# Row operations of two inverses on GpSimd, modulation's rows among the projections, and a written order for the recurrence's links

## The chip, the core and the metric

The kernel runs on one core of a Trainium2 chip. A core has four engines that compute: TensorE (PE, matrix products into PSUM), VectorE (DVE), ScalarE (ACT) and GpSimd (POOL); SyncE (SP) issues most of the loads. Each engine works through its own queue in order, and a semaphore holds an instruction until what it needs is there. The metric is the time of one execution on the device, in microseconds. Of the kernel before, three runs took 1595.9, 1590.84 and 1588.16 us; the median is 1590.84.

## The reference, cut to what matters

Two transformer blocks work one after the other on 512 tokens of width 1024, in float32. The change touches the first block alone, and in it the modulation, the projections and a recurrence over 256 context tokens and then 512 tokens:

```python
mod = silu(c) @ ada_w + ada_b                       # 6 x 1024 numbers: shifts, scales, gates
sh1, sc1, g1, sh2, sc2, g2 = split(mod, 6)
hx = rms_norm(x) * (1 + sc1) + sh1                  # the same for ctx
cb, cc, cx, r, k, v, w_lo, a_lo, g_lo = split(hx @ w_in)
for d in range(2):                                  # forward and backward in time
    decay = exp(-exp(-0.5) * sigmoid(w0[d] + tanh(w_lo) @ w_up[d]))
    a = sigmoid(a0[d] + a_lo @ a_up[d])
    k_d = k * (1 + (a - 1) * k_a)
    for t in time:                                  # S: 64 x 64, for each of 8 heads
        S = S * decay_t - (S @ kk_t) (kk_t * a_t)^T + v_t k_d_t^T
        y_t += S @ r_t
out = concat(cb * conv3(cc * cx), (groupnorm(y) + bonus) * gate) @ w_out
x = x + g1 * out
# then a gated convolutional FFN, the second block, a final norm
```

## The kernel before

Channels lie on the 128 partitions and tokens run along the free axis. A product with full float32 accuracy is made of three products of split operands (`mm3`, lines 169 to 171). A weight piece is loaded on SP's queue, copied by ScalarE to its high part `whi` and subtracted by VectorE to its low part `wlo` (`wsplit`, `split`, lines 181 and 182).

The work around the change has three stretches.

*Projections* (`proj`, about 45 to 260 us). `tile_of(u)` multiplies one block of 128 output columns of `w_in`, in two weight pieces of 512 rows each. The order is block 24, then 16 to 19 (`k`), 12 to 15 (`r`), then `v`, 25, and for each j of four the blocks 4+j, 8+j and j for the convolution. In between, the generator `prep` makes what the recurrence needs for head pair 0 and most of it for pair 1.

*Preparation and inverse* (`prep`, `inverse`). There are four head pairs j; 128 partitions hold the two heads of one. `prep(j)` computes decays and keys for direction 0 and then 1: products `pl` (lines 576, 577) through one PSUM buffer of tag `mm`, element operations on VectorE and ScalarE, and last the products `pa`, copied into the tile `AK` (line 636). `inverse(j)` then inverts 24 unit triangular matrices of 64 x 64, in blocks of 32: VectorE transposes `AK` to `U`; a loop over k of 31 rows makes one multiplication (line 671) and one subtraction (line 672) each on (31-k) x (k+1) elements of a partition; VectorE transposes the result `X` twice; products `pt` read `AK` again, products `po` follow (lines 691, 698 and 699), through one PSUM buffer of tag `inv`, and ScalarE copies `po` to `XT`. `AK` exists once, so the copies of the next pair into it wait until `pt` has read it.

*Recurrence* (`rwkv`, `stage`, about 260 to 520 us). A stage is one head pair. It goes through 12 chunks of 64 tokens in each of two directions d, each a chain of links: `pr` (product), `R` (ScalarE's copy, line 757), `pu` with `XT`, `U` (line 759), `p3`, and `S0` (line 769), the state which the next chunk's `pr` reads. From the fifth chunk on (the 512 tokens of the block itself) there is also `py`, the output, copied to `Y`. All four products of a direction go to parts of one PSUM bank, `C1[d]`. A helper `pair` makes, for two chunks at a time, the masked matrices (`psc`, to `AS` by VectorE, line 731) and transposed keys (`pkt`, to `kbt` by ScalarE). The group norm of a finished stage (`gn`) runs beside the next one; it starts with GpSimd's product `vt` x `bo` (line 789). Preparation's steps are put between the links by priorities; a planner orders each engine's queue by these and by what is ready. Where a tile's buffer is used again, the new tile waits for the old one's readers.

After stage 1 the preparation's memory is freed. Stages 2 and 3 then have `ada12` beside them (lines 528 to 542): the 4096 modulation numbers that the later parts need, as 32 products of a row of the transposed `ada_w` with `silu(c)`, each summed over 1024 elements by one VectorE operation (line 539), each row a load of 512 KB. Last, two groups of output products (`first`, `px`, 7 of 8 input blocks each) are issued beside the group norm of stage 3.

PSUM has eight banks. In the recurrence four are `sc` (`psc`, `pkt` and the group norm's products), two `C1`, one `mm` and one `inv`.

Of the kernel before, what the change touches and what calls it, by code (L numbers as in the profile page):

```python
# [122 lines left out]
class K:  # L123
# [10 lines left out]
    psa = None  # L134
# [38 lines left out]
    def psax(self, n=512, name="px"):  # L173
        return (self.psa or self.ps).tile([P, n], F32, tag="ax", name=name, bufs=self.axbufs)
# [124 lines left out]
    def proj(self):  # L299
# [45 lines left out]
        piece = lambda u, k0: self.wsplit(A["win"][u][:, k0:k0 + 4], 4, P)  # L345
# [108 lines left out]
        for j in range(4):  # L454
# [13 lines left out]
            for _ in range(self.RC):  # L468
                next(self.todo, None)

# [7 lines left out]
    def rwkv(self, es, ep):  # L478
# [4 lines left out]
        self.S0 = [st(f"S0{d}", [64]) for d in range(2)]  # L483
        self.C1 = [self.ps2.tile([P, 512], F32, name=f"c1{d}") for d in range(2)]
        for t in (*self.AS[0], *self.AS[1]):
            nc.vector.memset(t, 0.0)
        todo, gn = self.todo, iter(())
        for j in range(4):
            if j < 2:
                todo = chain(todo, self.prep(j + 2))  # L490
            gn = self.stage(j, self.S[j], todo, self.RB[j], gn)
            if j == 1:
# [26 lines left out]
    def first(self):  # L519
        self.ahead = []  # L520
        for n in range(2):
# [3 lines left out]
    def ada12(self):  # L525

        nc, wp = self.nc, self.wp
        tags = [("w", self.wbufs), ("whi", self.wsbufs), ("wlo", self.wsbufs)]
        cb, sb = (wp.tile([P, 1024], F32, tag=tags[i][0], name="cb", bufs=tags[i][1]) for i in (1, 2))
# [5 lines left out]
        for n in range(32):  # L535
            yield
            w, t = (wp.tile([P, 1024], F32, tag=tags[i][0], name="adaw", bufs=tags[i][1]) for i in (0, 2))
            nc.sync.dma_start(out=w, in_=self.A["adat"][n])
            nc.vector.scalar_tensor_tensor(out=t, in0=w, scalar=1.0, in1=cb, op0=ALU.mult, op1=ALU.mult, accum_out=acc[:, n:n + 1])
# [110 lines left out]
    def inverse(self, j):  # L650
# [14 lines left out]
        nc.gpsimd.memset(X.rearrange("p a b -> p (a b)")[:, ::33], 1.0)  # L665
        for k in range(31):
# [4 lines left out]
            nc.vector.tensor_tensor(out=tv, in0=U[:, k + 1:32, k:k + 1].to_broadcast([P, n, w]), in1=X[:, k:k + 1, 0:w].to_broadcast([P, n, w]), op=ALU.mult)  # L671
            nc.vector.tensor_tensor(out=X[:, k + 1:32, 0:w], in0=X[:, k + 1:32, 0:w], in1=tv, op=ALU.subtract)
# [12 lines left out]
        ps = lambda name: self.psp.tile([P, 12, 32], F32, tag="inv", name=name, bufs=1)  # L685
# [18 lines left out]
    def stage(self, j, S, todo, rb, gn):  # L704
# [5 lines left out]
        chunk = lambda d, g: g if d == 0 else (3 - g if g < 4 else 15 - g)  # L710
        cells = {}
        base = self.tc.cur_priority
        id2 = self.c("id2")

        def pair(i, d):

            c0 = min(chunk(d, 2 * i), chunk(d, 2 * i + 1))
            x = c0 >= 4
            W, N = (P, 192) if x else (64, 64)
            kr, kb = S["KR"][d], S["KB"][d]  # L720
            A = self.AS[d][i % 3]
            o = 256 + (c0 - 4) * P if x else c0 * 64
            ps = self.ps2.tile([P, 2, N], F32, tag="sc", name="psc", bufs=4)
            pt = self.ps2.tile([P, 2, 2, 64], F32, tag="sc", name="pkt", bufs=4)
            krs = [kr[:, o + c * W:o + c * W + W] for c in range(2)]
            for c in range(2):
                self.mmh(ps[:, c, 0:W], kb[:, c0 + c, d], krs[c])
                if x:
                    self.mmh(ps[:, c, W:N], kb[:, c0 + c, 1 - d], krs[c][:, 64:P])
            m = self.c(f"m{d}").bitcast(I32)[:, 0:N]  # L730
            nc.vector.copy_predicated(A[:, :, 0:N], m.unsqueeze(1).to_broadcast([P, 2, N]), ps)
            for c in range(2):
                for i in range(2):
                    self.mmh(pt[:, c, i], kb[:, c0 + c, i ^ d], id2)
            kt = r2.tile([P, 2, 2, 64], F32, tag="kbt", name="kbt", bufs=6)
            self.copy(nc.scalar, kt, pt)
            for c in range(2):
                cells[d, c0 + c] = (A[:, c], kt[:, c], krs[c], x)

        for g in range(12):  # L740
            at = base + self.PK * g
            with self.prio(at):
                if g % 2 == 0:
                    for d in range(2):
                        pair(g // 2, d)
                for d in range(2):
                    c = chunk(d, g)
                    A, kt, KR, x = cells.pop((d, c))
                    V, S0 = vt[:, c, :], self.S0[d]
                    R, U = (self.RU[d][g % 2][:, i, :] for i in range(2))  # L750
# [646 lines left out]
```

## Time and profile before

| | |
|---|---|
| three runs, median | 1590.84 us |
| the profiled execution | 1591.34 us, span 1589.5 us |
| busy in the span: PE, DVE, ACT, POOL | 94%, 63%, 40%, 8% |
| projections, 45 to 260 us: PE busy | 208.0 of 215 us |
| recurrence, 260 to 520 us: PE busy | 230.2 of 260 us |
| granted clock of TensorE over the span | 0.972 |

The span is the time from the first to the last instruction of the profiled execution; the execution itself takes 1.8 us more. Idle time of an engine counts only where another waits for it. Matrix products overlap in the engine, so a PE that is shown busy may still issue products more slowly than it could. In the rows below "waited for" is the event that came last; a wait for several events is put down to that one.

### The profile page before, as it was taken

The page shows a single profiled execution, that of the slowest core. Times are in us where ns is not written, and L with a number is a line of the kernel's source. Part 1 is how long each engine was busy: PE and PEld are TensorE (multiplying, and loading weights), DVE is VectorE, ACT ScalarE, POOL GpSimd, SP SyncE. Part 2 cuts the span into 40 slices and gives each one's busy share as a digit, 9 for nine tenths or more (in the row PEclk, how much of TensorE's full clock was granted, in tenths as well). Part 3 has the DMA queues.
Part 4 walks back from the last instruction along what each step waited for, and adds up shares of the span by engine and source line. Part 5 has one row for each costly group of instructions (what it writes and reads, how often), then busy time and mean ns, then how long its engine had stood idle before and what let it go on. Part 6 is the DMA issues. An engine that isn't in the chain of part 4 may idle for free. (4 is left out here: it accounts for less than half of the span.)

```text
span 1589.5 us, 28932 instructions
## 1 busy us (share of the span) xinstructions
PE 1498.6 (94%) x12062; PEld 1228.9 (77%) x12062; DVE 999.9 (63%) x1691; ACT 632.7 (40%) x1258; POOL 121.7 (8%) x141
## 2 busy tenths in 40 slices
PE   4899999989888999999999997999999999999998
PEld 2777787877777898888888875887677888888886
DVE  3436765777867669888863448588965555554221
ACT  3524343555453334333332325335554333333122
POOL 1111001020110000000000004121200000000000
PEclk9999898989999999999999998999999999999999
DMA  9243321010057613223323322211112222233221
GB/s 339 87 156 104 100 89 60 4 45 5 15 197 258 214 40 119 94 93 101 98 83 100 96 93 70 80 54 54 36 59 93 93 93 93 93 94 106 93 92 54
DMA packets 62179, 152.83 MB, mean 96 GB/s; under 512 B 12640, under 2 KB 14432, under 8 KB 62048
## 3 DMA queue, kind: packets, MB, share of 16 engines
q1 hardware_dynamic: 58016, 143.95, 27.9%
q10 hardware_dynamic: 4032, 7.04, 1.3%
q8 instruction: 94, 1.54, 0.4%
q14 instruction: 37, 0.30, 0.1%
HBM read 143.10 MB, written 7.86 MB: 95 GB/s over the span
## 5 line engine op out<-in xcount | busy, mean ns | idle before, releaser
L181 ACT ACTIVATE whi<-w 128x1024 fp32r<-128x1024 f32 (+2 forms) x220 | 208.7, 950 | 448.2 <-PE pm L170 333.3
L182 DVE TENSOR_TENSOR wlo<-w,whi 128x1024 fp32r<-128x1024 f32 (+2 forms) x212 | 229.9, 1086 | 201.3 <-ACT whi L181 195.3
L169 PE MATMUL pm<-ahi,whi 128*128 128x512 f32 (+1 forms) x624 | 236.4, 379 | 3.0 <-DVE sh L1080 2.6
L170 PE MATMUL pm<-alo,whi 128*128 128x512 f32 (+1 forms) x624 | 234.8, 376 | 0.0
L171 PE MATMUL pm<-ahi,wlo 128*128 128x512 f32 (+1 forms) x624 | 234.0, 375 | 0.0
L170 PE MATMUL pm<-al,whi 128*128 128x512 f32 x352 | 139.7, 397 | 0.0
L169 PE MATMUL pm<-ah,whi 128*128 128x512 f32 x352 | 139.2, 395 | 0.0
L171 PE MATMUL pm<-ah,wlo 128*128 128x512 f32 x352 | 139.2, 395 | 0.0
L169 PEld LDWEIGHTS pm<-ahi,whi 128*128 128x128 f32 x624 | 117.6, 189 | 24.2 <-ACT sh L1095 3.0
L171 PEld LDWEIGHTS pm<-ahi,wlo 128*128 128x128 f32 x624 | 117.6, 188 | 20.6 <-issue 0.7
L170 PEld LDWEIGHTS pm<-alo,whi 128*128 128x128 f32 x624 | 117.7, 189 | 20.3 <-issue 0.7
L953 DVE SCALAR_TENSOR_TENSOR cv<-pm,vec,cv 128x441 f32<-128x441 f32 (+2 forms) x176 | 121.1, 693 | 4.1
L170 PEld LDWEIGHTS pm<-al,whi 128*128 128x128 f32 x352 | 66.2, 188 | 16.1 <-issue 0.2
L171 PEld LDWEIGHTS pm<-ah,wlo 128*128 128x128 f32 x352 | 66.2, 188 | 16.1 <-issue 0.2
L169 PEld LDWEIGHTS pm<-ah,whi 128*128 128x128 f32 x352 | 66.2, 188 | 16.0
L171 PE MATMUL pm<-hhi,wlo 128*128 128x512 f32 x176 | 70.8, 402 | 2.7 <-DVE wlo L182 2.7
L169 PE MATMUL pm<-hhi,whi 128*128 128x512 f32 x176 | 71.4, 406 | 0.2 <-ACT whi L181 0.2
L170 PE MATMUL pm<-hlo,whi 128*128 128x512 f32 x176 | 70.6, 401 | 0.0
L169 PE MATMUL pd<-whi,gh 128*128 128x512 f32 x176 | 69.5, 395 | 0.0
L169 PE MATMUL pm<-hh,whi 128*128 128x512 f32 x176 | 69.3, 394 | 0.0
L170 PE MATMUL pm<-hl,whi 128*128 128x512 f32 x176 | 69.3, 394 | 0.0
L171 PE MATMUL pm<-hh,wlo 128*128 128x512 f32 x176 | 69.3, 394 | 0.0
(397 smaller groups left out, 3073.6 us busy)
## 6 DMA issues: line engine op xcount, KB each, us to landing
w<-in_fup SPq DMA_DIRECT2D x44, 512.0 KB, 3.7
adaw<-in_adat SPq DMA_DIRECT2D x32, 512.0 KB, 4.6
w<-in_win SPq DMA_DIRECT2D x44, 256.0 KB, 2.9
w<-in_wg SPq DMA_DIRECT2D x22, 512.0 KB, 3.6
w<-in_wu SPq DMA_DIRECT2D x22, 512.0 KB, 3.6
w<-in_wd SPq DMA_DIRECT2D x22, 512.0 KB, 3.7
w<-in_win SPq DMA_DIRECT2D x18, 512.0 KB, 3.5
w<-in_wout SPq DMA_DIRECT2D x16, 512.0 KB, 3.8
```

The costliest lines, as they stand in the source:

```text
L169: nc.tensor.matmul(out, lh, rh, start=(first and i == 0), stop=False)
L170: nc.tensor.matmul(out, lh, rl, start=False, stop=False)
L171: nc.tensor.matmul(out, ll, rh, start=False, stop=(last and i == n - 1))
L181: self.nc.scalar.activation(out=hi, in_=src, func=AF.Copy)
L182: (eng or self.nc.vector).tensor_tensor(out=lo, in0=src, in1=hi.bitcast(F32), op=ALU.subtract)
L953: nc.vector.scalar_tensor_tensor(out=o, in0=p[:, ro[0] + dr:ro[1] + dr, co[0] + dc:co[1] + dc], scalar=w(i), in1=o, op0=ALU.mult, op1=ALU.add)
```

## The change

It has six parts. They keep every product of the recurrence and every row operation.

- The loop of `inverse` runs on GpSimd for head pairs 2 and 3, and on VectorE for 0 and 1 as before.
- `ada12` moves into the projections: its first step and its 32 rows are drawn by `tile_of`, one for each of the blocks 12 to 24 and two for each of 25 and 0 to 11. Its tiles are a `cb` and two buffers `row` of its own. The second weight piece of blocks 0 to 11 and 25 gets its low part from GpSimd.
- `pair` becomes a generator `look` over all four stages. It is drawn by the links, eight steps ahead at the start and four for each chunk, so it also works on the next stage's chunks.
- All products of links and `look` carry one order token on PE, so they are issued in program order. In a chunk: `pr` of both directions, `R` of both, three steps of `look`, `pu` of both, `U` of both, the two parts of `p3` without `U`, one step of `look`, `p3` with `U`, the states, then `py`, whose copies to `Y` wait for the next chunk. The state gets two buffers a direction.
- `pr` and `p3` use the bank `C1[d]`, `pu` and `py` a second bank `C2[d]`. For the two banks, `sc` has three buffers instead of four, and the inverse's products share the one buffer of tag `mm` with preparation (the tag `inv` goes).
- Of the two early groups of output products, the second is issued at the start of the tail, in a bank of the next pool; tiles of tag `ax` alternate between the two pools.

```diff
-        return (self.psa or self.ps).tile([P, n], F32, tag="ax", name=name, bufs=self.axbufs)
+        pools = self.psa or [self.ps]
+        self.axn += 1
+        return pools[self.axn % len(pools)].tile([P, n], F32, tag="ax", name=name, bufs=self.axbufs // len(pools))
...
-        piece = lambda u, k0: self.wsplit(A["win"][u][:, k0:k0 + 4], 4, P)
+        piece = lambda u, k0: self.wsplit(A["win"][u][:, k0:k0 + 4], 4, P, eng=nc.gpsimd if k0 and not 12 <= u < 25 else None)
...
+        ada = self.ada12()
+
+        def rows(n):
+            for _ in range(n):
+                next(ada, None)
+
         def tile_of(u, x=True, c=True):
+            rows(1 if 12 <= u < 25 else 2)
...
+        for _ in ada:
+            pass
...
-        self.S0 = [st(f"S0{d}", [64]) for d in range(2)]
-        self.C1 = [self.ps2.tile([P, 512], F32, name=f"c1{d}") for d in range(2)]
+        self.S0 = [[st(f"S0{d}{i}", [64]) for i in range(2)] for d in range(2)]
+        self.C1, self.C2 = [[self.ps2.tile([P, 512], F32, name=f"c{i}{d}") for d in range(2)] for i in (1, 2)]
...
+        self.cells, self.vt, self.ahd = {}, {}, self.look()
+        self.load_v(0)
+        for _ in range(8):
+            next(self.ahd)
+        self.outs = []
...
-                todo = chain(self.splits(), self.ada12(), self.first())
+                todo = chain(self.splits(), self.first())
                 self.e3 = es.enter_context(ExitStack())
-                self.psa = self.psum(self.e3, "psa", side="right")
+                self.psa, self.axbufs = [self.psum(self.e3, "psa", side="right")], 1
...
-        for n in range(2):
+        for n in range(1):
...
-        tags = [("w", self.wbufs), ("whi", self.wsbufs), ("wlo", self.wsbufs)]
-        cb, sb = (wp.tile([P, 1024], F32, tag=tags[i][0], name="cb", bufs=tags[i][1]) for i in (1, 2))
+        row = lambda name: wp.tile([P, 1024], F32, tag="row", name=name, bufs=2)
+        cb, sb = wp.tile([P, 1024], F32, name="cb"), row("sb")
...
-            w, t = (wp.tile([P, 1024], F32, tag=tags[i][0], name="adaw", bufs=tags[i][1]) for i in (0, 2))
+            w = row("adaw")
...
+        e = nc.vector if j < 2 else nc.gpsimd
...
+            e.tensor_tensor(out=tv, in0=U[:, k + 1:32, k:k + 1].to_broadcast([P, n, w]), in1=X[:, k:k + 1, 0:w].to_broadcast([P, n, w]), op=ALU.mult)
+            e.tensor_tensor(out=X[:, k + 1:32, 0:w], in0=X[:, k + 1:32, 0:w], in1=tv, op=ALU.subtract)
...
-        ps = lambda name: self.psp.tile([P, 12, 32], F32, tag="inv", name=name, bufs=1)
+        ps = lambda name: self.psp.tile([P, 12, 32], F32, tag="mm", name=name, bufs=1)
...
+    def look(self):
+
         nc, r2 = self.nc, self.r2
-        XT = S["XT"]
-        vt = r2.tile([P, 12, 64], F32, tag="vt", name="vt", bufs=2)
-        nc.sync.dma_start(out=vt, in_=self.vD[:, j])
+        id2 = self.c("id2")
+        for j in range(4):
+            for i in range(6):
+                S = self.S[j]
+                x = i >= 2
+                W, N = (P, 192) if x else (64, 64)
+                part = []
+                for d in range(2):
+                    c0 = min(self.CH(d, 2 * i), self.CH(d, 2 * i + 1))
+                    kr, kb = S["KR"][d], S["KB"][d]
+                    o = 256 + (c0 - 4) * P if x else c0 * 64
+                    part.append((c0, kb, [kr[:, o + c * W:o + c * W + W] for c in range(2)], self.AS[d][i % 3]))
+                for d, (c0, kb, krs, A) in enumerate(part):
+                    ps = self.ps2.tile([P, 2, N], F32, tag="sc", name="psc", bufs=3)
+                    for c in range(2):
+                        if c:
+                            yield
+                        self.mmh(ps[:, c, 0:W], kb[:, c0 + c, d], krs[c], order="pe")
+                        if x:
+                            self.mmh(ps[:, c, W:N], kb[:, c0 + c, 1 - d], krs[c][:, 64:P], order="pe")
+                    m = self.c(f"m{d}").bitcast(I32)[:, 0:N]
+                    nc.vector.copy_predicated(A[:, :, 0:N], m.unsqueeze(1).to_broadcast([P, 2, N]), ps)
+                    yield
+                for d, (c0, kb, krs, A) in enumerate(part):
+                    pt = self.ps2.tile([P, 2, 2, 64], F32, tag="sc", name="pkt", bufs=3)
+                    for c in range(2):
+                        if c:
+                            yield
+                        for n in range(2):
+                            self.mmh(pt[:, c, n], kb[:, c0 + c, n ^ d], id2, order="pe")
+                    kt = r2.tile([P, 2, 2, 64], F32, tag="kbt", name="kbt", bufs=6)
+                    self.copy(nc.scalar, kt, pt)
+                    for c in range(2):
+                        self.cells[j, d, c0 + c] = (A[:, c], kt[:, c], krs[c])
+                    yield
...
+        def fill(n):
+            for _ in range(n):
+                next(self.ahd, None)
+
+        def put():
+
+            if self.outs:
+                self.copy(nc.scalar, *self.outs.pop(0))
 
         for g in range(12):
             at = base + self.PK * g
+            x, vt = g >= 4, self.vt[j]
             with self.prio(at):
+                cs = [self.CH(d, g) for d in D]
+                A, kt, KR = zip(*[self.cells.pop((j, d, cs[d])) for d in D])
+                V = [vt[:, c, :] for c in cs]
+                R, U = ([self.RU[d][g % 2][:, i, :] for d in D] for i in range(2))
+                old, new = ([self.S0[d][(g + i) % 2] for d in D] for i in range(2))
+
+                pr, p3 = ([self.C1[d][:, i * 64:i * 64 + 64] for d in D] for i in range(2))
+                pu, py = ([self.C2[d][:, i * 64:i * 64 + 64] for d in D] for i in range(2))
+                for d in D:
+                    mm(pr[d], A[d][:, 0:64], V[d], True, g == 0)
                     if g:
+                        mm(pr[d], KR[d][:, 0:64], old[d], False, True)
+                put()
+                for d in D:
+                    nc.scalar.activation(out=R[d], in_=pr[d], func=AF.Copy)
+                put()
+                fill(3)
+                for d in D:
+                    mm(pu[d], XT[:, 12 * d + cs[d], :], R[d])
+                for d in D:
+                    nc.scalar.activation(out=U[d], in_=pu[d], func=AF.Copy, scale=-1.0)
+                if g < 11:
+                    for d in D:
+                        mm(p3[d], kt[d][:, 0], V[d], True, False)
                         if g:
+                            mm(p3[d], id2, old[d], False, False)
+                fill(1)
+                if g < 11:
+                    for d in D:
+                        mm(p3[d], kt[d][:, 1], U[d], False, True)
+                    for d in D:
+                        nc.scalar.activation(out=new[d], in_=p3[d], func=AF.Copy, scale=PC[d][:, cs[d]:cs[d] + 1])
+                if x:
+                    for d in D:
+                        mm(py[d], A[d][:, 64:P], V[d], True, False)
+                        mm(py[d], KR[d][:, 64:P], old[d], False, False)
+                        mm(py[d], A[d][:, P:192], U[d], False, True)
+                        self.outs.append((Y[d][:, cs[d] - 4, :], py[d]))
+                if g == 11:
+                    put()
+                    put()
+                if g == 8 and j < 3:
+                    self.load_v(j + 1)
...
+            self.psa.append(self.ps)
+            self.axbufs = 2
+            self.ahead.append((self.psax(), self.wsplit(A["wout"][1], KD, P)))
+            self.mm3(self.ahead[1][0], [(*self.ahead[1][1](k), self.ahi[k], self.alo[k]) for k in range(7)], last=False)
```

## Rows read from the trace of the kernel before

**Rows 1.** The page, part 1: busy us, share of the span, instructions.
```profile
PE 1498.6 (94%) x12062; PEld 1228.9 (77%) x12062; DVE 999.9 (63%) x1691; ACT 632.7 (40%) x1258; POOL 121.7 (8%) x141
```

**Rows 2.** Windows: stretch, length, busy us (count) PE, PEld, DVE, ACT, POOL, clock, DMA, GB/s.
```profile
197.00:260.00 63.00, 62.87 (x347) 50.35 (x347) 38.51 (x53) 26.40 (x42) 3.15 (x11) 1.00 0.28 88
...
260.00:331.00 71.00, 64.76 (x1499) 55.13 (x1496) 50.77 (x107) 38.55 (x131) 8.50 (x17) 0.88 0.11 33
...
460.00:520.00 60.00, 51.50 (x1202) 44.25 (x1197) 45.12 (x82) 25.74 (x108) 4.95 (x4) 0.95 0.76 254
```

**Rows 3.** Timeline in stage 3: start, us, engine, line, output<-inputs, count.
```profile
495.14 0.28 PE L638 MATMUL c<-RU,kbt 64*64 64x64 f32 x4
...
495.60 0.28 PE L638 MATMUL c<-S,KR 64*64 64x64 f32 x4
...
496.04 0.30 ACT L769 ACTIVATE S<-c,pc 128x64 f32<-128x64 f32 x1
```

**Rows 4.** Timeline of GpSimd: the product that follows stage 2 and stage 3.
```profile
464.29 1.04 POOL L789 TENSOR_TENSOR vt<-vt,bo 128x512 f32<-128x512 f32 x1 [23.34 <-issue]
...
517.17 1.04 POOL L789 TENSOR_TENSOR vt<-vt,bo 128x512 f32<-128x512 f32 x1 [38.74 <-PE c L638]
```

**Rows 5.** Waits, 445 to 521 us: who waited for whom, us, times, longest.
```profile
ACT S L769 <- PE c L638: 20.1, 24, 2.2
...
DVE adaw L539 <- DMA adaw<-in_adat: 13.7, 15, 2.1
```

**Rows 6.** Tile `X`, inverses 0 and 1: ns min/median/max, first and last start.
```profile
L672 DVE TENSOR_TENSOR X<-X,tmp x31: 192/358/427, 155.6 to 182.1; 128x31 f32<-128x31 f32 x2, 128x60 f32<-128x60 f32 x2, 128x87 f32<-128x87 f32 x2, 128x112 f32<-128x112 f32 x2
...
L672 DVE TENSOR_TENSOR X<-X,tmp x31: 192/359/425, 265.4 to 304.8; 128x31 f32<-128x31 f32 x2, 128x60 f32<-128x60 f32 x2, 128x87 f32<-128x87 f32 x2, 128x112 f32<-128x112 f32 x2
```

**Rows 7.** Tile `po`, inverses 1 and 3: the copies that end an inverse.
```profile
L188 ACT ACTIVATE zx<-po x4: 479/481/483, 314.1 to 315.6; 32x384 f32<-32x384 f32 x4
...
L188 ACT ACTIVATE XT<-po x4: 479/481/482, 443.5 to 445.0; 32x384 f32<-32x384 f32 x4
```

**Rows 8.** Tile `adaw`: the 32 products of the modulation.
```profile
L539 DVE SCALAR_TENSOR_TENSOR adaw<-adaw,cb x32: 1212/1225/1227, 451.9 to 515.6; 128x1024 f32<-128x1024 f32 x32
L539 DVE DVE_READ_ACCUMULATOR adaw<-adaw,cb x32: 80/82/86, 453.1 to 516.7; 128x1 f32 x32
```

**Rows 9.** Groups on VectorE, 197 to 260: busy us, mean ns, idle before.
```profile
L182 DVE TENSOR_TENSOR wlo<-w,whi 128x512 fp32r<-128x512 f32 x18 | 12.4, 687 | 3.8 <-ACT whi L181 3.8
...
L462 DVE TENSOR_TENSOR u<-zx,pm 128x512 f32<-128x512 f32 x4 | 2.8, 690 | 6.0 <-PE pm L171 6.0
```

**Rows 10.** Lines on GpSimd, whole span: ns min/median/max, first and last start.
```profile
L808 POOL TENSOR_TENSOR ys<-Y x3: 1261/1262/1262, 332.8 to 465.3; 128x512 f32<-128x512 f32 x3
...
L182 POOL TENSOR_TENSOR wlo<-w,whi x8: 2361/2369/2433, 981.3 to 1117.5; 128x1024 fp32r<-128x1024 f32 x8
...
L601 POOL COPY pc<-cs x8: 198/329/640, 134.9 to 392.6; 128x12 f32<-128x12 f32 x8
```

**Rows 11.** Tile `AK`: copies into it for pair 0, then for pair 2.
```profile
L188 ACT ACTIVATE AK<-pa x4: 492/493/494, 136.6 to 149.5; 128x384 f32<-128x384 f32 x4
...
L188 ACT ACTIVATE AK<-pa x3: 490/490/490, 313.1 to 327.0; 128x384 f32<-128x384 f32 x3
```

**Rows 12.** Line 568, 125 to 151 us: the first copy of preparation 0.
```profile
L568 ACT ACTIVATE bo<-pb x1: 177/177/177, 127.1 to 127.1; 128x8 f32<-128x8 f32 x1
```

**Rows 13.** Timeline after stage 3: last copy to `Y`, first `pm` product.
```profile
517.36 0.22 ACT L188 ACTIVATE Y<-c 128x64 f32<-128x64 f32 x1 [0.67 <-PE c L638]
...
533.96 0.39 PE L169 MATMUL pm<-ahi,whi 128*128 128x256 f32 x1
```

**Rows 14.** Timeline, 332 to 335 us: GpSimd and VectorE side by side.
```profile
332.84 1.26 POOL L808 TENSOR_TENSOR ys<-Y 128x512 f32<-128x512 f32 x1
...
332.98 1.20 DVE L671 TENSOR_TENSOR tmp<-U,X 128x60 f32<-128x60 f32 x1
...
334.22 0.22 DVE L672 TENSOR_TENSOR X<-X,tmp 128x60 f32<-128x60 f32 x1
```

More of the change, by code (lines that the diff above doesn't have):

```diff
@@ L133 @@
     RB, RC = (4, 2, 1, 1), 5
-    psa = None
+    psa, axn = None, 0
     def __init__(self, tc, A):
@@ L490, in rwkv @@
                 todo = chain(todo, self.prep(j + 2))
-            gn = self.stage(j, self.S[j], todo, self.RB[j], gn)
+            gn = self.stage(j, todo, self.RB[j], gn)
             if j == 1:
@@ L702, in inverse @@
             self.copy(nc.scalar, XT[b1[h], D[1], 0:32], po[b1[h]], -1.0)
-    def stage(self, j, S, todo, rb, gn):
+    CH = staticmethod(lambda d, g: g if d == 0 else (3 - g if g < 4 else 15 - g))
+    def look(self):
         nc, r2 = self.nc, self.r2
-        XT = S["XT"]
-        vt = r2.tile([P, 12, 64], F32, tag="vt", name="vt", bufs=2)
-        nc.sync.dma_start(out=vt, in_=self.vD[:, j])
+        id2 = self.c("id2")
[33 more added lines that the diff above has]
+                    yield
@@ L709, in stage, with load_v @@
+    def load_v(self, j):
+        vt = self.r2.tile([P, 12, 64], F32, tag="vt", name="vt", bufs=2)
+        self.nc.sync.dma_start(out=vt, in_=self.vD[:, j])
+        self.vt[j] = vt
+    def stage(self, j, todo, rb, gn):
+        nc, r2 = self.nc, self.r2
+        XT, PC = self.S[j]["XT"], self.S[j]["PC"]
         Y = [r2.tile([P, 8, 64], F32, tag=f"Y{d}", name="Y", bufs=1) for d in range(2)]
-        chunk = lambda d, g: g if d == 0 else (3 - g if g < 4 else 15 - g)
-        cells = {}
         base = self.tc.cur_priority
@@ L713, in stage @@
         id2 = self.c("id2")
[L715 to L738, printed above, removed]
@@ L740, in stage @@
+        mm = lambda *a: self.mmh(*a, order="pe")
+        D = range(2)
+        def fill(n):
[4 more added lines that the diff above has]
+                self.copy(nc.scalar, *self.outs.pop(0))
         for g in range(12):
             at = base + self.PK * g
+            x, vt = g >= 4, self.vt[j]
             with self.prio(at):
-                if g % 2 == 0:
-                    for d in range(2):
-                        pair(g // 2, d)
@@ L746, in stage @@
[L746 to L750, printed above, removed]
-                    pr, pu, py, p3 = (self.C1[d][:, i * 64:i * 64 + 64] for i in range(4))
-                    mm = lambda *a: self.mmh(*a, order=f"c1{d}")
-                    mm(pr, A[:, 0:64], V, True, g == 0)
-                    if g:
-                        mm(pr, KR[:, 0:64], S0, False, True)
-                    nc.scalar.activation(out=R, in_=pr, func=AF.Copy)
-                    mm(pu, XT[:, 12 * d + c, :], R)
-                    nc.scalar.activation(out=U, in_=pu, func=AF.Copy, scale=-1.0)
-                    if g < 11:
-                        mm(p3, kt[:, 0], V, True, False)
-                        if g:
-                            mm(p3, id2, S0, False, False)
-                        mm(p3, kt[:, 1], U, False, True)
-                    if x:
-                        mm(py, A[:, 64:P], V, True, False)
-                        mm(py, KR[:, 64:P], S0, False, False)
-                    if g < 11:
-                        nc.scalar.activation(out=S0, in_=p3, func=AF.Copy, scale=S["PC"][d][:, c:c + 1])
-                    if x:
-                        mm(py, A[:, P:192], U, False, True)
-                        self.copy(nc.scalar, Y[d][:, c - 4, :], py)
@@ L778, in stage @@
         self.tc.cur_priority = base + 12 * self.PK
-        return self.gn(j, Y, S["bo"], vt)
+        return self.gn(j, Y, self.S[j]["bo"], self.vt[j])
     def gn(self, j, Y, bo, vt):
@@ L789, in gn @@
         nc.gpsimd.tensor_tensor(out=bv, in0=bv, in1=wide(bo), op=ALU.mult)
-        pv = self.ps2.tile([P, 8, 64], F32, tag="sc", name="pv", bufs=4)
+        pv = self.ps2.tile([P, 8, 64], F32, tag="sc", name="pv", bufs=3)
         for i in range(8):
@@ L798, in gate @@
         def gate():
-            pg = self.ps2.tile([P, NX], F32, tag="sc", name="pg", bufs=4)
+            pg = self.ps2.tile([P, NX], F32, tag="sc", name="pg", bufs=3)
             nc.tensor.matmul(pg, gup, self.sg, start=True, stop=True)
@@ L826, in gn @@
         yield
-        py = self.ps2.tile([P, 8, 64], F32, tag="sc", name="py", bufs=4)
+        py = self.ps2.tile([P, 8, 64], F32, tag="sc", name="py", bufs=3)
         for i in range(8):
```

4 lines of the change are left out of this document (1 added, 3 removed).

## The prediction

> **What bounds the kernel now.** I read the page's shares first: TensorE is busy 94% of the span [rows 1], so time can only come from stretches where it is busy and yet not at its pace. The windows by stage come next [rows 2]. The projections (197 to 260 us) show PE 62.9 of 63 us at full clock: nothing to win there, only to lose. In the recurrence (260 to 520) PE is busy 86 to 91% in the first and the last stage, and that share misleads: its short matmuls overlap, so I turn to the timeline for their pace. Four records make one 64-column product, and five products start 0.46 us apart from first to last, 0.115 us each [rows 3]. One head pair's stage has 182 products in the links (46 for `pr`, 24 `pu`, 64 `p3`, 48 `py`), 104 ahead of them (56 `psc`, counting 128 columns as two, 48 `pkt`) and 16 in the group norm: 302 x 0.115 = 34.7 us. The last stage takes 52.9 us (464.3 to 517.2) [rows 4]. So 18 us of it are waits. The list of waits names them: ScalarE's state copy behind PE, 20.1 us, and VectorE behind the modulation's loads, 13.7 us [rows 5]. One case shows the first: the last product of `p3` starts at 495.14, but the copy `S` starts at 496.04, after the four `py` products that go to the same PSUM bank [rows 3].
>
> Beside the links a second chain runs, and it is as long: each pair's inverse needs its predecessor's to be done. Inverse 1's row operations last from 265.4 to 305.0 [rows 6], its result is copied out by 316.1; inverse 3's by 445.5 [rows 7]. Stage 3 starts 18.8 us later, so today the links, not the inverses, set the end.
>
> **The change, part by part.** Durations come from the profiled execution, 1591.3 us (span 1589.5), 0.5 us over the median of the three runs; the sum is made against it.
>
> *Modulation's rows.* 32 products of 1.225 us, with some 0.08 to read the sum, leave the stretch 452 to 517 and go between the projections' tiles [rows 8], one each for 9 tiles, two each for the last 13. About 24 fall into 197 to 260: 24 x 1.305 = 31.3 us on VectorE, which has 38.5 of 63 busy there [rows 2]. The second halves of 13 weight pieces (0.687 each, 8.9 us) go to GpSimd [rows 9]. VectorE gets to 60.9 of 63. Loads: 24 x 0.52 MB on top of 88 GB/s gives about 288 GB/s, where stage 3 shows 254 at most over a long stretch [rows 2]. Each load waits on SP for one of two row buffers, and the weight pieces of the next tile are queued behind it; PE waits for those. A row buffer is held for a load and a product, so if rows are late, tiles are late. Cost: nothing if VectorE and SP keep up, 12 us if each of the 12 tiles is late by 1 us; I take 3, nearer to nothing, because rows that slip can end under stage 0, where nobody needs them.
>
> *Row operations of inverses 2 and 3 on GpSimd.* 62 instructions each, 31 multiplications and 31 subtractions, of 31x1, 30x2 ... elements: 5,456 elements a kind. GpSimd's two-input operation takes 1.262 us for 512 elements and 2.369 for 1024: 2.16 ns an element and 0.155 fixed [rows 10]; with a broadcast operand it is 1.04 for 512 [rows 4], 1.73 ns an element. So 62 x 0.155 + 5.456 x (1.73 + 2.16) = 9.6 + 21.2 = 30.8, with 0.05 between two instructions 34 us. No row shows runs of one to 31 elements. Lower bound 27 us, what VectorE takes undisturbed (155.6 to 182.3) [rows 6]; upper 62 x 0.329 (the small copy) + 10.912 x 2.16 = 44 [rows 10], 50 with a penalty for short runs. I take 34, from the nearest rows. Queued behind them on GpSimd are the group norm's three operations, whose reader is not late.
>
> *One PSUM slot for preparation and inverse.* The tag `inv` becomes `mm`, with one buffer. Now preparation 2's first direction runs while inverse 1 is worked on; in its last piece the copy to `AK` waits until the inverse has read `AK` (313.1) [rows 11]. With one slot the next preparation's first product must wait for the copies of the previous inverse. So the chain becomes serial. Its period: preparation 23 us undisturbed (127.1 to 150.0) [rows 11, 12], 25 with links beside it; 5.6 to the first row operation (150.0 to 155.6); 34; then 11.1 for transposes, block products and copies (305.0 to 316.1) [rows 6, 7]. Sum 75.7 us. Start: inverse 1 stays on VectorE. It took 39.6 us, of which 27 is its own; without preparation 2 among it I take 31, between the two. 265.4 + 31 + 11.1 = 307.5, with the 3 us above 310.5. Inverse 2 is out at 386.2, inverse 3 at 461.9.
>
> *Links.* With `pr`, `p3` in one bank and `pu`, `py` in another, the state copy no longer waits for `py`; both chains alternate in a written order; two state buffers allow `py` to come last. `pu` of stage j waits for inverse j in PE's queue, and everything of the links and the look-ahead is queued behind it, read by ScalarE. Stages 0 and 1 get shorter, but end in that wait: their gain costs nothing and gives nothing. Only stage 3 counts: lower bound 34.7 us (the pace), upper 52.9 (as now). I take 42, nearer to the pace, since both large waits go; the rest is for split copies that come due when the preparation's memory is freed, and for a start after idleness. (PE's granted clock over the last stage is 0.95 already [rows 2].)
>
> *After it.* One of two groups of 21 products for the output projection is still issued beside the last group norm; the other needs a bank of the next pool. Now 16.6 us pass from the last `Y` copy to the first `pm` product [rows 13]; both groups lie in it, so the moved one costs 8 us at most, if PE stands still in its place; in return the group norm no longer queues behind the modulation's products on VectorE (two end there, 2.6 us [rows 8]). I take 0, from -3 to +8.
>
> **Sum.** Stage 3 ends at 461.9 + 42 = 503.9 instead of 517.2: -13.3 us. 1591.3 - 13.3 = **1578 us**; from the median it would be 1577.5.
>
> **A rule against the change.** In the trace a GpSimd sum runs from 332.84 to 334.10; a VectorE operation on 60 elements issued beside it takes 1.20 us and ends 0.08 us behind it, the next one on 60 elements takes 0.22 [rows 14]. So the two exclude each other. The Trainium skill, SBUF — State Buffer, "Who interferes with whom", states that a VectorE instruction with two SBUF inputs and a GpSimd instruction that reads SBUF share an interface as an exclusive lock. The trace agrees; by the rule the sum would be rival B's, without it the forecast's.
>
> **Rivals.**
> A (slower): GpSimd's row operations are slow and the serial chain sets the end. Each us goes in twice. At 50 us: +32, 1610 us. It decides from 41 us a set on (13.3 / 2 above 34). For it: 1- to 31-element runs, no row of them. Against: large operations keep 2.16 ns steadily.
> B (no change): the exclusion shown above hits the projections. VectorE's work of 60.9 us has 2.8 us twice that reads PSUM (one of the two stands in [rows 9]) and 1.9 us of accumulator reads; the other 53 and GpSimd's 13 x 1.26 = 16.4 make 70 in 63 us. PE is late by 7 to 10 us rather than 3: 1582 to 1585. Against: late rows may drift under stage 0.
> C (much faster): preparation still overlaps the inverse before it, because the slot is free while row operations run. 11 us less, twice: 1556. Against: a preparation that held the slot until `AK` is free would stop the inverse that frees it.
> D (the change does not do what it says): the written order gives no shorter stage 3, 52.9 us: 1589.
>
> **How the numbers follow.** About 0.5%, 8 us, is what this kernel's runs can tell from none (three runs lie 7.7 us apart). Forecast 0.38, A 0.22, B 0.18, C 0.14, D 0.08. The forecast's own range is 1566 to 1590 (row operations 28 to 40 us, stage 3 from 37 to 48). Faster: 0.32 of the forecast, C's 0.14, 0.04 of B: 0.50. Same: 0.06 + 0.14 + 0.07 = 0.27. Slower: A and 0.01 of D: 0.23. The range that holds 8 in 10 reaches to C's side at 1548 and past A at 1612.
>
> **What would show it.** Right: GpSimd's 62 operations take 30 to 38 us a set; preparation 2's first `pl` starts after inverse 1's last copy; PE stands still before the first `pu` of stages 2 and 3; stage 3 lasts 38 to 46 us; PE stays over 60 of 63 us in the projections. Wrong: `pl` of preparation 2 during inverse 1 (C); sets of over 41 us (A); a recurrence that begins 8 us later (B); a stage 3 that starts without waiting, for then the links still set the end.

## The result and the profile after

The changed kernel takes 1631.45 us (median of four runs, 1627.61 to 1635.69), the kernel before 1589.5 beside it: ratio 1.026, interval 1.022 to 1.030. The forecast was 1578, the range ended at 1612.

The page of the changed kernel, part 1, and its windows by stage (stretch, length, busy us with counts of PE, PEld, DVE, ACT, POOL, clock, DMA, GB/s):

```profile
PE 1493.1 (91%) x12062; PEld 1236.5 (76%) x12062; DVE 960.7 (59%) x1554; ACT 631.5 (39%) x1258; POOL 211.6 (13%) x278
```

```profile
197.00:260.00 63.00, 59.01 (x489) 46.94 (x490) 39.09 (x49) 26.79 (x45) 17.12 (x22) 0.91 0.29 92
...
351.00:444.00 93.00, 64.53 (x1506) 58.21 (x1504) 34.12 (x45) 38.02 (x130) 47.20 (x83) 0.74 0.04 13
444.00:525.00 81.00, 51.74 (x1348) 48.88 (x1344) 23.49 (x35) 33.88 (x120) 39.05 (x69) 0.75 0.17 53
525.00:565.00 40.00, 39.08 (x1089) 35.72 (x1087) 10.38 (x20) 22.27 (x98) 3.88 (x4) 1.00 0.02 6
```

Stages 1 and 2 of the kernel before, in the same view:

```profile
331.00:405.00 74.00, 67.60 (x1548) 57.26 (x1550) 56.90 (x118) 39.96 (x135) 12.61 (x17) 0.91 0.03 9
405.00:460.00 55.00, 46.30 (x1197) 41.04 (x1195) 41.65 (x93) 27.45 (x98) 3.58 (x5) 0.94 0.24 79
```

PE is 5 us less busy than in [rows 1] and the span is 44 us longer: time spent standing still, and it is in stages 1 and 2. They last 45 us longer (351 to 525, before 331 to 460), and PE is idle in them for 58 us instead of 15. The granted clock is lower there too (0.74 and 0.75, before 0.91 and 0.94). Stage 3 is what was hoped for: PE is busy 39.1 of 40 us, at clock 1.00.

The timeline of the stall in stage 1 (start, us, engine, line, output<-inputs, count, idle before and what ended it). The link's copy `R` came at 381.64; its `pu` (`c<-RU,zx`) starts at 402.83:

```profile
381.60 0.72 PE L654 MATMUL psc<-KR,KB 64*64 64x128 f32 x10
...
396.50 0.25 POOL L689 TENSOR_TENSOR X<-X,tmp 128x31 f32<-128x31 f32 x1
396.78 1.90 DVE L691 STREAM_TRANSPOSE F<-X 128x1024 f32<-128x1024 f32 x1 [18.82 <-POOL X L689]
398.55 1.89 DVE L692 STREAM_TRANSPOSE F<-X 128x1024 f32<-128x1024 f32 x1
...
400.50 1.22 PE L708 MATMUL pt<-F,AK 32*32 32x32 f32 x38 [18.18 <-DVE F L692]
...
402.83 0.42 PE L654 MATMUL c<-RU,zx 64*64 64x64 f32 x2
```

Inverse 2's `pt` stands in PE's queue between two links of stage 1. It waits for VectorE's transposes `F`, those for GpSimd's last row. Nothing in that link needs inverse 2. From one `R` to the next of the same direction pass 29.6 us there. In stage 2, where inverse 3's `pt` stands, 31.6 us pass; three to four are usual. The waits there, 466 to 505 us (who for whom, us, times, longest):

```profile
PE pt L708 <- DVE F L692: 17.5, 1, 17.5
DVE F L691 <- POOL X L689: 15.7, 1, 15.7
```

In the kernel before, PE waited 1.2 us for inverse 3's `F`:

```profile
PE pt L691 <- DVE F L675: 1.2, 1, 1.2
```

Tile `X` and the copies from `po` after (ns min/median/max, first and last start), for [rows 6] and [rows 7]:

```profile
L688 POOL TENSOR_TENSOR tmp<-U,X x62: 238/550/1085, 356.8 to 484.4; 128x31 f32<-128x31 f32 x4, 128x60 f32<-128x60 f32 x4, 128x87 f32<-128x87 f32 x4, 128x112 f32<-128x112 f32 x4
...
L691 DVE STREAM_TRANSPOSE F<-X x4: 1900/1902/1911, 197.2 to 485.0; 128x1024 f32<-128x1024 f32 x4
```

```profile
L190 ACT ACTIVATE XT<-po x8: 480/482/483, 408.9 to 498.0; 32x384 f32<-32x384 f32 x8
```

Inverse 3 is out at 498.4, not 445.5. The product `vt` on GpSimd, which follows a stage's last link, marks where stage 3 begins and ends ([rows 4] before: 464.29, 517.17):

```profile
524.39 1.04 POOL L849 TENSOR_TENSOR vt<-vt,bo 128x512 f32<-128x512 f32 x1 [33.12 <-issue]
...
564.42 1.05 POOL L849 TENSOR_TENSOR vt<-vt,bo 128x512 f32<-128x512 f32 x1 [32.39 <-PE c L654]
```

Stage 3 lasts 40.0 us instead of 52.9, but begins 60 us later.

### The profile page after: what moved, and what is told of

Its sections match the earlier page's. It is cut to its first block, busy times and chain, and to the rows that moved or that the text cites. A ratio compares the mean times of both kernels' runs of the same rounds, so it can differ in the third digit from the quotient of the medians.

```text
span 1633.9 us, 29054 instructions
## 1 busy us (share of the span) xinstructions
PE 1493.1 (91%) x12062; PEld 1236.5 (76%) x12062; DVE 960.7 (59%) x1554; ACT 631.5 (39%) x1258; POOL 211.6 (13%) x278
## 5 line engine op out<-in xcount | busy, mean ns | idle before, releaser
L184 DVE TENSOR_TENSOR wlo<-w,whi 128x1024 fp32r<-128x1024 f32 (+2 forms) x199 | 220.5, 1109 | 168.5 <-ACT whi L183 166.7
L171 PEld LDWEIGHTS pm<-ahi,wlo 128*128 128x128 f32 x624 | 118.0, 189 | 21.1 <-issue 0.7
L170 PE MATMUL pd<-wlo,gh 128*128 128x512 f32 x176 | 69.5, 395 | 0.0
L171 PE MATMUL pd<-whi,gl 128*128 128x512 f32 x176 | 69.5, 395 | 0.0
```

The costliest lines, as they stand in the source:

```text
L170: nc.tensor.matmul(out, lh, rl, start=False, stop=False)
L171: nc.tensor.matmul(out, ll, rh, start=False, stop=(last and i == n - 1))
L184: (eng or self.nc.vector).tensor_tensor(out=lo, in0=src, in1=hi.bitcast(F32), op=ALU.subtract)
```

## Experiments

**1. Rows of all inverses on VectorE.**

```diff
-        e = nc.vector if j < 2 else nc.gpsimd
+        e = nc.vector
```

> The changed kernel with the row operations of all four inverses on VectorE; modulation's rows, the written links and the banks stay. Theory 1 (the 42 us are two sums: some 16 us because the recurrence starts late, and some 26 us because pt of inverses 2 and 3 stands in the middle of the links in PE's queue and waits there for GpSimd's rows): VectorE's rows end some 9 us earlier a set, pt stands later in the queue, the two stalls of 29.6 and 31.6 us shrink to under 12 us each, stage 3 starts near 500 instead of 524.7, and the time is 1600 to 1610. Theory 2 (only the length of the chain of sets counts, GpSimd's rows lie 40 us in it instead of 31): 2 x 9 us, 1613. Theory 3 (the written order of links is what loses): 1630, no change.

1587.83 us, 0.999 of before (0.998 to 1.000): 44 us less than the changed kernel, more than either theory gave. The 62 operations of inverses 2 and 3 take 31 and 29 us from first to last (40 and 41 on GpSimd), inverse 3 is out at 469.6, no link step of stages 1 and 2 is over 11.2 us, stage 3 begins at 480.2. Theory 3 falls.

**2. Modulation's rows and splits back in their old place, GpSimd's rows kept.**

```diff
-            rows(1 if 12 <= u < 25 else 2)
-                todo = chain(self.splits(), self.first())
+                todo = chain(self.splits(), self.ada12(), self.first())
```

> The changed kernel with modulation's rows and the low-part splits put back (the rows after stage 1, on the weights' buffers, all splits of the projections on VectorE); GpSimd's rows of the inverses and the written links stay. Theory 1: the first link is back at 266 instead of 282, so -16 us, and stage 3 gets the rows back that it had before (39 us would become 45 to 52): 1620 to 1628. Theory 2 (the late start is the weight of GpSimd's and the links' own instructions, not of the rows): the start stays at 282 and stage 3 gets longer, 1635 to 1645.

1633.11 us, no gain, between the two theories. Both halves of theory 1 show, and the second eats most of the first: the first link is 17.6 us earlier (264.3 for 281.9), stage 3 lasts 14 us more (52.0 from first to last `R`, 37.9 in the changed kernel).

**3. Both undone: written links, two banks and the shared slot alone.** (Both edits above.)

> Both of the two edits before undone at once: only the written order of links, two banks for each chain and the shared PSUM slot are left of the change. Theory 1: the gains of the two runs add up, first link at 266, stalls in the links under 12 us, stage 3 from some 484: 1585 to 1598, level with the kernel before. Theory 3 (the written order itself costs, since links and look-ahead wait in one queue): over 1600.

1602.80 us, 1.009 of before (1.006 to 1.013), over theory 1's range: slower than experiment 1 by 15 us, though its first link comes 13.7 us earlier (263.7 for 277.4). Waits of the links-only kernel, 505 to 545 us (who for whom, us, times, longest):

```profile
PEld px L169 <- ACT whi L183: 10.4, 1, 10.4
PE px L169 <- ACT whi L183: 9.5, 1, 9.5
ACT whi L183 <- DMA w<-in_wout: 7.1, 4, 3.1
```

The first row comes at 458 here, after inverse 3 is out (452), as in the kernel before (452 after 445.5); all need 64 us, to 522; stage 3 ended at 511, and the output projection's weights came behind the rows. In the kernel before both ended at 517 [rows 4, 8]. In the profiled runs 1086 us follow stage 3 here, 1069 in experiment 1 and 1074 in the kernel before. So here the shorter links pay only if the rows are out of that stretch.

**4. The kernel before, with GpSimd's rows alone.**

```diff
+            e = nc.vector if j < 2 else nc.gpsimd
-            nc.vector.tensor_tensor(out=tv, in0=U[:, k + 1:32, k:k + 1].to_broadcast([P, n, w]), in1=X[:, k:k + 1, 0:w].to_broadcast([P, n, w]), op=ALU.mult)
+            e.tensor_tensor(out=tv, in0=U[:, k + 1:32, k:k + 1].to_broadcast([P, n, w]), in1=X[:, k:k + 1, 0:w].to_broadcast([P, n, w]), op=ALU.mult)
...
```

> The kernel before with one edit alone: GpSimd does the row operations of inverses 2 and 3. Its inverses have a PSUM slot of their own, so preparations overlap, and its links have the old order. Theory 1 mended (F waits for GpSimd in VectorE's queue and pt in PE's, links stand behind both; in the changed kernel these rows cost 44 us): the links of stages 1 and 2 get steps of over 20 us here too, and the time is 1605 to 1630. Theory 2 (they cost so much only because the shared PSUM slot makes the sets serial): preparation 3 still overlaps, and the loss is under 10 us, up to 1600.

1627.86 us, 1.024 (1.021 to 1.027). Preparations overlap here, so the shared slot is not needed for the loss. Its waits, 365 to 460 us:

```profile
PE pt L692 <- DVE F L676: 22.8, 2, 13.9
...
DVE gm L812 <- POOL ys L809: 18.2, 1, 18.2
ACT RU L760 <- PE c L638: 17.5, 6, 16.3
DVE F L675 <- POOL X L673: 17.3, 2, 15.7
...
PE pv L638 <- POOL vt L790: 15.4, 1, 15.4
```

The same two waits, and a third: the group norm's `vt` and `ys` stand behind the rows in GpSimd's queue, and PE stands still for `pv`.

**5. The kernel before, with modulation's rows alone.** (Experiment 2's diff the other way round; all splits of the projections stay on VectorE.)

> The kernel before with one edit alone: modulation's rows among the projections. The first link goes from 266 to 278-282 (+12 to +16), and the stretch that the rows leave, 452 to 517 beside stage 3, gets shorter: in the changed kernel stage 3 lasts 38 us without them, here 52 with them. If the two cancel as they did in the two runs with GpSimd's rows: 1586 to 1594. If the rows were hidden where they stood, as the prediction's rival D has it: 1600 to 1606.

1589.58 us, 1.000 (0.998 to 1.003), no change. The first link comes at 273.9, 7.8 us later than before and not 12 to 16; stage 3 is 50.2 us long, 2.7 less. The rest of the balance lies behind stage 3: in the profiled run, the fastest of ten, 1062.9 us follow it instead of 1074.2.

**6. GpSimd's rows, `pt` and `po` given a place.** The end of inverses 2 and 3 is written behind the last link of the stage before and joins the links' order. With it preparation 3 moves into stage 2, and the preparation's memory is freed after stage 2.

```diff
+            m = nc.tensor.matmul(*a, start=True, stop=True)
+            if order:
+                self.tc.stamp_issue_order_token(m.ins, order)
```

> The changed kernel with pt and po of inverses 2 and 3 given a place in the written order: behind the last link of the stage before instead of in its middle; GpSimd still does the rows, and all matmuls are the same. For that preparation 3 is written in stage 2 and its room is given up after stage 2. Theory 1: links of stages 1 and 2 run to their end while GpSimd works, the steps of 29.6 and 31.6 us vanish from the middle of the stages, inverse 3 still ends near 498 and stage 3 starts there: -26 us, 1602 to 1608. Theory 2: the chain of sets sets the end, nothing changes: 1628 to 1634.

1617.48 us: 14 us less than the changed kernel, of the 26 expected. A step of 24.1 us stays in stage 1. Waits, 377 to 402 us:

```profile
DVE F L694 <- POOL X L692: 20.8, 1, 20.8
ACT kbt L190 <- PE pkt L657: 20.3, 2, 19.5
PEld pkt L657 <- DVE AS L766: 18.7, 1, 18.7
```

PE no longer waits for `pt`. Now `F` waits in VectorE's queue, the masked copies `AS` of the look-ahead stand behind it, and PE waits for those.

**7. The same, with `F` placed too**, behind the `AS` copies.

```diff
+        F1, F2 = big("F1"), big("F2")
...
+            if j >= 2:
+                self.tc.stamp_issue_order_token(f.ins, "dv")
...
-                    nc.vector.copy_predicated(A[:, :, 0:N], m.unsqueeze(1).to_broadcast([P, 2, N]), ps)
+                    f = nc.vector.copy_predicated(A[:, :, 0:N], m.unsqueeze(1).to_broadcast([P, 2, N]), ps)
+                    self.tc.stamp_issue_order_token(f.ins, "dv")
```

> As the run before with pt and po placed (GpSimd still does the rows of inverses 2 and 3), and VectorE's two transposes F of these inverses also placed: behind the masked copies AS that serve the links of the stage before. Theory 1, mended (a link stands behind GpSimd's rows through two in-order queues: PE's, where pt stands, and VectorE's, where F waits for X and the AS copies stand behind it; the run with pt alone placed still had a step of 24 us, and F waited 20.8 us): the steps over 15 us vanish from stages 1 and 2, preparation 3 starts near 413 instead of 424, inverse 3 ends at 495 to 498, stage 3 starts there, and the time is 1601 to 1608. Theory 2 (the chain of sets with GpSimd's 40 us in it is what costs, wherever F and pt stand): no better than the run with pt placed, 1614 to 1620.

1596.69 us, 1.004 of before (1.002 to 1.006): 35 us less than the changed kernel with the same arithmetic on the same engines. No step of stage 1 is over 9.1 us, none of stage 2 over 6.9, inverse 3 is out at 493.2, stage 3's first `R` comes at 493.9. That is 4 us below the range expected. PE's wait for `F`, 350 to 494 us, and that first `R`:

```profile
PE pt L711 <- DVE F L705: 23.7, 2, 22.4
```

```profile
493.90 0.34 ACT L826 ACTIVATE RU<-c 128x64 f32<-128x64 f32 x2
```

PE still waits, but now at the end of stage 2, where the forecast had put the wait, and stage 3 starts when inverse 3 is out.

**8. VectorE's rows, only inverse 3's end placed.** (Experiments 1 and 7, with `j >= 3`.)

> Rows of all inverses on VectorE, and F, pt and po of inverse 3 alone placed behind stage 2's links. With the rows on VectorE and no placing, inverse 3 ended at 469.1, but stage 2's last steps were 9.6 and 10.9 us and stage 3 began at 480.5. Theory 1: stage 2 ends before inverse 3 does, stage 3 begins at 469 to 474, 1577 to 1582, faster than the kernel before. Rival (VectorE is now short of time: the placed order makes the row operations later by what it frees): 1587, no change.

1583.54 us, 0.994 (0.993 to 0.996), between theory 1 and its rival. Stage 2's last two steps are 3.1 and 2.7 us, and stage 3's first `R` comes right after inverse 3 is out (475.8; 476.5). Inverse 3 itself is out 6 us later than in experiment 1.

**9. VectorE's rows, the projections' splits on VectorE too.**

```diff
-        piece = lambda u, k0: self.wsplit(A["win"][u][:, k0:k0 + 4], 4, P, eng=nc.gpsimd if k0 and not 12 <= u < 25 else None)
+        piece = lambda u, k0: self.wsplit(A["win"][u][:, k0:k0 + 4], 4, P)
```

> Rows of all inverses on VectorE, and the low-part splits of the projections back on VectorE; modulation's rows stay among the projections. The first link was at 277 to 282 with rows and GpSimd splits, at 264 with neither. If the two engines' exclusion of each other makes the late start (prediction's rival B), the start falls to 266 to 270 and the time to 1577 to 1581. If the rows' transfers and VectorE's time make it, GpSimd's splits were a help and the start goes to 280 to 290: 1590 to 1600.

1588.29 us, experiment 1's time; first link at 277.3, as there. So neither: the splits' engine makes no difference to the time.

**10. Experiment 8 with modulation's rows held off inverse 0**: each row and the `F` of inverse 0 go into VectorE's written order.

```diff
-            rows(1 if 12 <= u < 25 else 2)
+            rows(2 if u >= 12 else 1)
...
+            self.tc.stamp_issue_order_token(f.ins, "dv")
...
-            if j >= 3:
+            if j in (0, 3):
                 self.tc.stamp_issue_order_token(f.ins, "dv")
```

> The best version so far (rows of the inverses on VectorE, tail of inverse 3 placed) with modulation's rows kept out of preparation 0's inverse: none between its first transpose U and its transposes F. Theory S1 (the 13.6 us by which the first link is late are one step at 167 to 190 us: some ten row products of 1.3 us stand in VectorE's queue between the operations of inverse 0, and the projections' matmuls behind its pt in PE's queue): the first link moves from 277-282 to 266-271 and the time to 1571 to 1576. Theory S2 (the lateness follows from the 32 rows wherever they stand: 41 us of VectorE and 16.8 MB of transfers in the projections): the lateness moves to a later tile and the time stays at 1581 to 1585.

1582.82 us, no gain over 1583.54. Without rows (experiment 3) and with them (experiment 1), the windows of 180 to 200 us were as follows (stretch, length, busy us with counts of PE, PEld, DVE, ACT, POOL, clock, DMA, GB/s):

```profile
180.00:190.00 10.00, 6.62 (x200) 5.20 (x198) 4.93 (x6) 3.41 (x7) 1.94 (x4) 0.65 0.33 109
190.00:200.00 10.00, 10.00 (x42) 7.86 (x40) 4.55 (x7) 4.24 (x9) 0.14 (x2) 0.84 0.35 116
```

```profile
180.00:190.00 10.00, 5.83 (x24) 4.12 (x22) 9.21 (x26) 2.57 (x5) 0.00 (x0) 0.87 0.64 184
190.00:200.00 10.00, 3.73 (x79) 2.94 (x81) 9.69 (x18) 1.09 (x3) 3.16 (x5) 0.50 0.27 106
```

There most of the lateness did arise: `pt` of inverse 0 waited 7.2 us for `F` (2.3 without rows). With the rows held it waits 4.3 and the step at 167 to 190 is gone, but against experiment 3 the projections slip 6.5 us at 93 to 99, where rows now come in closer order, and 7.4 at 190 to 205. S2 fits: in both places that were tried the rows cost about as much.

**11. Experiment 8 with a PSUM slot of their own for `pt` and `po`**, at the look-ahead's cost.

```diff
-        ps = lambda name: self.psp.tile([P, 12, 32], F32, tag="mm", name=name, bufs=1)
+        ps = lambda name: self.psp.tile([P, 12, 32], F32, tag="inv", name=name, bufs=1)
...
-                    ps = self.ps2.tile([P, 2, N], F32, tag="sc", name="psc", bufs=3)
+                    ps = self.ps2.tile([P, 2, N], F32, tag="sc", name="psc", bufs=2)
```

> The best version so far with a PSUM slot of their own for pt and po again (the bank is taken from the look-ahead: its slots go from 3 to 2). If the shared slot makes the chain of sets serial (the prediction's base case, against its rival C), preparation 3 starts before inverse 2 ends, as it did in the kernel before (bo 332.8 to 334.5 there against 379.6 to 398.7 with one slot), inverse 3 ends 10 us or more before 470, and stage 3 begins at stage 2's end, near 464: 1571 to 1576. If two slots for the look-ahead are too few, the links' steps grow by about 1 us each (48 of them): 1590 to 1620.

1577.39 us, 0.993 (0.990 to 0.996): faster than both kernels, 1.4 us above the range expected. Against experiment 8 (0.993 to 0.996) the gain is not clear of the noise. The first copies of the four preparations with the slot shared (experiment 8), and with two slots:

```profile
L587 ACT ACTIVATE bo<-pb x4: 177/177/178, 129.9 to 398.7; 128x8 f32<-128x8 f32 x4
```

```profile
L587 ACT ACTIVATE bo<-pb x4: 178/178/178, 129.3 to 339.5; 128x8 f32<-128x8 f32 x4
```

Preparation 3 begins 59 us earlier, inverse 3's rows end at 434.7, and stage 3's first `R` comes at 462.8 instead of 476.5. The sets were serial by the shared slot.

**12. Experiment 11 without the placing.**

> The run with a PSUM slot of their own for pt and po (rows of all inverses on VectorE, two slots for the look-ahead), without the placing of F, pt and po of inverse 3. There inverse 3's rows ended at 434.7, but F stood behind the AS copies of stage 2's links, stage 2 ended at 450 and stage 3 began at 462.8. Theory A (with the sets overlapping, placing the tail late is now what stage 3 waits for): pt goes into the links again, stage 3 begins at 452 to 457, and the time is 1566 to 1573. Theory B (pt and po in the middle of stage 2 hold the links up by as much as they come earlier): 1575 to 1582, no better.

1580.03 us, 0.992 (0.990 to 0.995), level with experiment 11, as theory B has it. One link step of stage 2 takes 20.5 us, and stage 3's first `R` comes at 471.9 instead of 462.8. Not all of that step is the inverse's: PE waits 3.7 us in it for `F`, and besides `pt` and `po` products of the group norm and of the output projection stand in it, one of which waits 1.8 us for its weights.

## Why the prediction was wrong

In the profiled executions the forecast, 1578.0, and the result, 1635.7, are 57.7 us apart. By the forecast's own terms (a period in brackets):

| Term | Forecast | Measured | Off by |
|---|---|---|---|
| inverse 1 out | 310.5 | 321.9 | +11.4 |
| inverse 2 out, a period later | 386.2 (75.7) | 410.9 (89.0) | +13.3 |
| inverse 3 out | 461.9 (75.7) | 498.4 (87.5) | +11.8 |
| from there to stage 3 | 0 | 26.0 | +26.0 |
| stage 3 | 42 | 40.0 | -2.0 |
| rest, against before | 0 | -2.8 | -2.8 |

*The step that failed* is "Stages 0 and 1 get shorter, but end in that wait: their gain costs nothing and gives nothing. Only stage 3 counts." I let `pu` of the next stage wait at a stage's end and never asked where the inverse's own `pt` and `F` stand in the queues of PE and VectorE. They stand in the middle of a stage, and all links behind them wait for GpSimd. Stage 2 then still had six chunks to do after the one that inverse 3's `pt` held up, so stage 3 began 26 us after inverse 3 was out; one of the forecast's own signs of being wrong came true, a stage 3 "that starts without waiting, for then the links still set the end". Experiments 6 and 7 show it: with the same arithmetic on the same engines, these instructions placed later gave 14 and 35 us back. (Preparation 3 moved with them; no run separates that.) In the kernel before PE waited only 1.2 us at that place: VectorE did the rows itself, and `F` followed them at once.

*The other terms* were too small as well: the first three lines of the table are 36.5 us. Inverse 1's rows began 12.6 us late (281.0, forecast 265.4 + 3) and took 4.0 less; the rows of inverses 2 and 3 took 13.4 more, the ends of the three inverses 8.1 more, the two preparations 6.4 more. With the placing mended and these terms as they are, experiment 7 takes 1596.69 us: above the forecast, but inside the range that ends at 1612. So it was the place of `pt` and `F` that led out of it.

*GpSimd's rows, 34 us.* The forecast had 30.8 us busy and 3.1 between the operations. Busy they were 33.7 and 33.1 us. From the first to the end of the last they take 40.0 and 41.4, since 0.08 us, not 0.05, lies between two of them (about 4.6 us in all) and the group norm's operations stand among them (1.7 and 4.0 us). The Trainium skill, GPSIMD Engine Reference, "Elementwise — side-by-side cycle accounting", has an addition of 2048 elements take 1.96 times as long as on VectorE; here, with 31 to 256 elements, busy time is 33.7 against 21.1 for inverse 1, 1.6 times. Rival A priced this length alone: at the measured lengths 6.0 + 7.4 = 13.4 us, under a quarter of the 57.7. That the reader of the group norm behind them "is not late" fails in experiment 4, where `pv` waits 15.4 us.

*The period, 75.7.* Serial, as said: preparation 2's first `pl` starts at 324.7, after inverse 1's last copy, so C falls; with a slot of their own for `pt` and `po` (experiment 11) preparations overlap again. Rows make 6 to 7 us of what the period is longer; from an inverse's end to the next one's first row pass 34.9 and 32.7 us instead of 30.6, and the end takes 13 to 14 instead of 11.1. With VectorE's rows (experiment 1) the periods are 77 and 75.

*Modulation's rows, 3 us* (0 to 12). The first link comes 13.7 us late (experiments 1 and 3), 16 in the changed kernel, 7.8 with the old links (experiment 5). I put some 24 of the 32 rows at 197 to 260 and looked for lateness there. But they start at 57.6 us, 29 of them before 197:

```profile
L555 DVE SCALAR_TENSOR_TENSOR adaw<-adaw,cb x32: 1204/1224/2282, 57.6 to 211.3; 128x1024 f32<-128x1024 f32 x32
```

So VectorE is busy 39.1 of 63 us at 197 to 260, not 60.9, and the loads are 92 GB/s, not 288; most of the lateness arises earlier, beside preparation 0. PE's 59.0 of 63 us misses the sign "over 60", and the first link is later than B's sign of 8 us. But B's exclusion between the splits on GpSimd and VectorE is not the cause (experiment 9). The Trainium skill, SBUF — State Buffer, "Who interferes with whom", has a VectorE instruction with two SBUF inputs contend with a GpSimd instruction that reads SBUF; what this may cost the projections does not show in experiment 9's time. The return in stage 3 was in the forecast's 42: with the new links, rows out of stage 3 shorten it by 10 us (39.8 in experiment 1, 49.8 in experiment 3, from `vt` to `vt`). What was missed is that they also free the weights' loads after it.

*Links and tail.* Stage 3 at 40.0 for 42 and the tail at -2.8 (from -3 to +8) were right; D falls.

So of the three edits GpSimd's rows alone cost 2.4%, the written links with their banks and the shared slot 0.9%, modulation's rows alone nothing; modulation's rows and links together (experiment 1) also nothing, since the rows' going lets the shorter stage 3 count. What the exact sum of lateness in the projections is made of stays open: experiment 10 moved it and did not remove it, and between two profiles with the same projections the first link differs by up to 5 us (277.4 and 282.5 in experiments 1 and 8).

## What to carry to other kernels

Before work goes to a slower engine, look up who consumes its result and what stands behind that consumer in its own queue. Here that wait, and not the length of the work, was most of the price: placing the consumers gave back 35 of the 44 us that undoing the move gave. When independent work is written in between a chain, give the instructions that end it a place where they are ready; with VectorE's shorter rows this brought some 4 us (experiment 8) or nothing clear (experiment 12). And a gain in one stage can be lost to transfers that hold up the next one (experiment 3).

## What was not expected of the hardware

Between two small dependent operations GpSimd leaves 0.08 us (median), VectorE 0.03 (inverse 1). An operation on 31 elements a partition takes 0.25 to 0.27 us on GpSimd in 31 runs of one element and 0.24 to 0.25 in one run of 31 (VectorE, inverse 1: 0.13 to 0.20). So short runs bring no penalty of the kind that the upper bound of 50 us had in mind.
